# Two-layer hybrid encoder trunk on one core: an opening with a VectorE cast, another product order and shorter warming, the factor's spread in another PSUM tile, and the last stores in parts

## The chip, the core and the metric

The kernel runs on one core of one Trainium2 chip. A core has five engines with a program each: TensorE (PE) multiplies matrices into PSUM, VectorE (DVE) and ScalarE (ACT) work on whole tiles, GpSimd (POOL) does small things, and SyncE (SP) issues transfers. An engine does its instructions in the order in which they stand in its program; a semaphore makes it wait for another engine or for a DMA. The metric is the device time of one execution in microseconds (us), as a median of several runs.

## The reference, cut to what matters

Two layers, each with a mixer and a ConvGLU feed-forward part, and a root-mean-square norm before and behind each of the four sub-layers. `x` is one sequence of 512 tokens with 1024 features, in float32.

```python
for layer in range(DEPTH):                       # DEPTH = 2
    h = rms_norm(x, mix_pre_norm[layer])
    m = even_mixer(h, ...) if layer == 0 else odd_mixer(h, ...)
    x = x + rms_norm(m, mix_post_norm[layer])
    h = rms_norm(x, ffn_pre_norm[layer])
    x = x + rms_norm(conv_ffn(h, ...), ffn_post_norm[layer])
# rms_norm(t, g) = t * rsqrt(mean(t*t, features) + 1e-6) * g
# even_mixer: h @ w_in, latent attention | 2-D neighbourhood attention, @ w_out
# odd_mixer:  h @ w_in, retention both ways | long convolution by FFT, @ w_out
# conv_ffn:   (gelu(dwconv3(h @ w_gate)) * (h @ w_up)) @ w_down   (1024 -> 2816 -> 1024)
```

## The kernel before

**Layout.** `x` is held transposed: eight tiles of 128 features by 512 tokens. Every float32 operand of a large product is split in a high part (`hi`, the value rounded to the type that PE multiplies at full speed) and a low part (`lo`, what the rounding left), and `mm` issues three products for each pair: hi by hi, hi by lo, lo by hi. A product of a 128x128 stationary tile with a 128x512 moving one adds into one PSUM bank.

**Weights** come in pieces of 128x1024 (512 KB). `load_weight` has SP issue the transfer to one of two `raw` buffers, ACT cast it to `whi` and DVE subtract to `wlo`; four pairs of these exist, so three pieces can wait ready (`AHEAD = 3`). The first piece of all comes in two halves.

**Norms.** The norm's factor is not applied to the input of a projection but to its result: `stats` sums the squares over the features with products by a column of ones, VectorE adds the epsilon, POOL takes the power -0.5; the result is a factor for each token, in columns (`rcol`). `spread` turns it into a tile `Rb` in which every row holds the factors: four PE transposes into one PSUM tile, and a copy by ACT. What multiplies by `Rb` waits for that copy.

**PSUM** has eight banks, given out in turn under four names: three "pj" and two "A" take the large products, two "B" the transposes and the sums, and one "C" what is left over. A bank is written anew when its reader has finished.

**The opening** (`main`). PE first multiplies a column of ones by itself `WARM` = 14 times, with no use for the result. Then `x` and the first four weight pieces are loaded in turn, ACT and DVE scale and split `x` to `h` (`scaled`) and square it (L544; DVE sums the squares, L546), and `proj_tok` does the first projection: eight pieces `k` of the features by four token tiles, three products each.

**Between two sub-layers** `boundary` drains the last products, takes the norm behind, updates `x`, and runs the first four projections of the next sub-layer (`proj_halves`) while the norm in front of it is not ready yet. At its end (L446 to L449) it issues the `stats` for the next factor behind the last of these products, spreads the factor and copies it to `Rb`; that copy is `self.hold`, behind which later weight casts are issued.

**The odd mixer** (`mixer1`) reads that `Rb`: VectorE scales the four projections of the boundary by it (L1079), then come twelve more projections, each scaled as it ends. Between them stands the filter's `spectrum` (L1012): eight groups of six products, all into the one "C" bank. ACT copies the first four groups out (`sp`, L1033), VectorE the other four. The feed-forward parts (`ffn`) read `Rb` in the same way; the first one also permutes it (`Rp`, L875) and turns it back to columns with four small products (L878).

**Order.** The program is not written in the order in which it runs: a tile scheduler reorders each engine's instructions by its own planned times, by priorities (`high_priority`), and by `issue_after`, which keeps an instruction behind another. The last boundary writes the output: each of the eight tiles in two halves of 256 tokens, issued on SP for odd `k` and on ACT for even `k` (L397).

Of the kernel before, what the change touches and what calls it, by code (L numbers as in the profile page):

```python
# [12 lines left out]
AF = mybir.ActivationFunctionType  # L13
# [3 lines left out]
P = 128  # L17
S = 512
D = 1024
KT = D // P  # L20
# [14 lines left out]
C_MPRE, C_MPOST, C_FPRE, C_FPOST = 0, 16, 32, 48  # L35
# [169 lines left out]
class Body:  # L205
# [44 lines left out]
    def load_weight(self, n=1):  # L250
        nc = self.nc
        raw = self.wp.tile([P, 1024], F32, tag="raw", bufs=2, name=self.nm("raw"))
        hi = self.wp.tile([P, 1024], F32R, tag="whi", name=self.nm("whi"))
        lo = self.wp.tile([P, 1024], F32R, tag="wlo", name=self.nm("wlo"))
        for i in range(n):
            c = slice(i * 1024 // n, (i + 1) * 1024 // n)
            nc.sync.dma_start(raw[:, c], self.I["w"][self.wi][:, c])
            with self.tc.high_priority(WP):

                with self.tc.issue_after(self.hold) if self.hold is not None else ExitStack():  # L260
                    nc.scalar.copy(hi[:, c], raw[:, c])  # L261
                nc.vector.tensor_tensor(lo[:, c], raw[:, c], hi[:, c].bitcast(F32), ALU.subtract)  # L262
        self.wi += 1
        self.wq.append((hi, lo))
# [23 lines left out]
    def stats(self, accs, dim, n=S, e=None, out=None):  # L288
        nc = self.nc
        c = n // P  # L290
        ps = self.PS("B")
        for j in range(c):
            for a in accs:
                nc.tensor.matmul(ps[:, j:j + 1], a[:, j * P:(j + 1) * P], self.ones, start=a is accs[0], stop=a is accs[-1])  # L294
        v = self.small(4, "v")[:, :c]
        if e is None:
            nc.vector.tensor_scalar(v, ps[:, :c], 1.0 / dim, EPS, ALU.mult, ALU.add)
        else:
            nc.vector.scalar_tensor_tensor(v, ps[:, :c], 1.0 / dim, e, ALU.mult, ALU.add)
        r = self.small(4, "r")[:, :c] if out is None else out  # L300
        self.pow = nc.gpsimd.tensor_tensor(r, v, self.mhalf[:, :c], ALU.pow)
        return r
# [29 lines left out]

    def scaled(self, hl, src, g, cs):
        hi, lo = hl[0][:, cs], hl[1][:, cs]
        self.nc.scalar.activation(hi, src, AF.Copy, scale=g)
        self.nc.vector.scalar_tensor_tensor(lo, src, g, hi.bitcast(F32), ALU.mult, ALU.subtract)


# [2 lines left out]
    def boundary(self, pool, tag, x, prod, gpost, gpre, ns, ftag, perm=False, rin=None):  # L341
        nc = self.nc
# [47 lines left out]
        def update(cs, R):  # L390
            v = v3 if perm else (lambda a: a)
            for k in range(KT):
                f = fs[k][:, cs]
                nc.vector.tensor_tensor(f, f, R, ALU.mult)
                (nc.gpsimd if last and k in POOLK else nc.vector).tensor_tensor(v(f), v(f), own(k, cs), ALU.add)
                if last:
                    (nc.sync if k % 2 else nc.scalar).dma_start(self.out[k * P:(k + 1) * P, cs], f)  # L397
                    continue
                self.scaled(h[k], f, self.col(gpre + k), cs)

# [22 lines left out]
        g = products(cb)  # L423
        next(g)
        if not last:
            acc2 = new("acc2")
            h = self.new_h()
# [10 lines left out]
        g = self.proj_halves(h, ("pj", "A", "pj", "A"))  # L438
# [7 lines left out]
        with self.tc.issue_after(self.last_mm):  # L446
            with self.tc.high_priority(HP):
                self.stats([acc2], D, out=self.rcol)
            self.hold = nc.scalar.copy(self.Rb, self.spread(self.rcol, "C")).ins  # L449
        return fs, h, ps  # L450

    def gemm(self, ps, w, h, cs=slice(0, S), order=tuple(range(KT))):
# [22 lines left out]
        return ps  # L475


    def proj_tok(self, h, at={}):
        ps = [self.PS(t) for t in ("pj", "pj", "A", "A")]
        for q in range(4):  # L480
            w = self.weight()
            for kk in range(2):
                k = 2 * q + kk
                if k in at:
                    at[k]()
                for j in range(4):
                    js = slice(j * P, (j + 1) * P)
                    self.mm(ps[j], (h[k][0][:, js], h[k][1][:, js]), self.wslice(w, slice(kk * 512, kk * 512 + 512)),
                            k == 0, k == KT - 1)
        return ps  # L490

    def out_proj(self, a, order):
# [31 lines left out]
    def main(self):  # L524
# [12 lines left out]
                self.load_weight(2 if k == 0 else 1)  # L537
        h = self.new_h()
        with self.phase("l0") as p:
            for k in range(KT):  # L540
                self.scaled(h[k], x[k], self.col(C_MPRE + k), slice(0, S))
            sqs = [self.X("sq", tag="xb") for _ in range(KT)]
            for k in range(KT):
                nc.scalar.activation(sqs[k], x[k], AF.Square)  # L544
                if k:
                    nc.vector.tensor_tensor(sqs[0], sqs[0], sqs[k], ALU.add)  # L546
            x, h, pre = self.mixer0(p, h, sqs[0])
# [10 lines left out]
    def mixer0(self, p, h, acc):  # L558
# [20 lines left out]
        def value_mm(ops, v, hd, pt, start, stop):  # L579
# [4 lines left out]
        nv = []  # L584
        self.new_factor()
        pss = self.proj_tok(h, {6: lambda: self.stats([acc], D, out=self.rcol),
                                7: lambda: nc.scalar.copy(self.Rb, self.spread(self.rcol))})
        self.table = self.pow.ins
        loads()
        rcol, Rb = self.rcol, self.Rb  # L590
# [698 lines left out]
AHEAD = 3  # L1289
HP = 100  # L1290
WP = 5
WARM = 14
LATE = 7
SB = {"xa": 8, "xb": 8, "qk": 8, "t3": 8, "s": 3}
NS = 4
# [28 lines left out]
```

## Time and profile before

| | |
|---|---|
| median of three runs | 1290.13 us (1288.92 to 1290.34) |
| the profiled execution, its own time | 1291.72 us |
| its span, from the first instruction to the last | 1289.9 us |
| mean granted clock of TensorE, as a share of full speed | 0.996 |
| PE busy | 1266.4 us, 98% of the span, 6366 matmuls |
| DVE busy | 806.1 us, 62% |
| ACT busy | 588.5 us, 46% |
| DMA, mean over the span | 105 GB/s |

Busy times are those of one engine; two engines that are busy at once count twice. A matmul's record covers its whole way through the engine, so neighbouring records overlap: what a product costs in a dense stretch is the distance from one start to the next, not the length of its record. An idle time in brackets behind a row is how long the engine stood still before it, and what ended that.

### The profile page before, as it was taken

What the parts mean: (1) busy time and instruction counts of PE and PEld (TensorE: products, weight loads), DVE (VectorE), ACT (ScalarE), POOL (GpSimd) and SP (SyncE); (2) the same over time, 40 slices, a digit from 0 to 9 for tenths busy, and PEclk for the clock granted to TensorE, in tenths of its full rate; (3) what the DMA queues carried; (4) which work ended last, traced back from release to release, by engine and by line L of the source; (5) the groups of instructions that cost most, each with busy time, mean ns of one, the idle gap of its engine ahead of it and who ended that gap; (6) DMA issues with size and microseconds to landing.
All of it is one profiled execution on the core that took longest, in us unless ns stands there. A gap on an engine that the chain in (4) does not pass through costs nothing.

```text
span 1289.9 us, 16429 instructions
## 1 busy us (share of the span) xinstructions
PE 1266.4 (98%) x6366; PEld 1054.1 (82%) x6366; DVE 806.1 (62%) x1289; ACT 588.5 (46%) x953; POOL 67.1 (5%) x81
## 2 busy tenths in 40 slices
PE   9999899999999999999999999999999999999997
PEld 8887677998788788888988888778988888888886
DVE  6678897479866765322587796873875555552323
ACT  6455798556543333222443265544553333332221
POOL 1000222000000000000110000010000000000002
PEclk9999999999999999999999999999999999999998
DMA  7432012223435343333383233214243332333331
GB/s 237 131 96 81 1 34 82 85 84 99 132 127 165 131 131 98 98 114 99 113 284 112 90 119 98 66 34 131 66 132 98 98 98 94 93 95 112 99 99 66
DMA packets 43786, 135.99 MB, mean 105 GB/s; under 512 B 4955, under 2 KB 7195, under 8 KB 43196
## 3 DMA queue, kind: packets, MB, share of 16 engines
q1 hardware_dynamic: 36156, 116.52, 28.9%
q0 software_dynamic: 3664, 12.06, 2.9%
q10 hardware_dynamic: 3888, 6.36, 1.4%
q8 instruction: 50, 0.82, 0.3%
q14 instruction: 28, 0.23, 0.1%
HBM read 126.53 MB, written 8.39 MB: 105 GB/s over the span
## 4 chain that ended last, share of the span: by engine, by line
PE 89%; ACT 4%; DVE 3%; issue 2%; DMA 1%; POOL 1%; SPq 0%; ACTq 0%; DVEq 0%; POOLq 0%
PE pspj L282 17%; PE pspj L284 17%; PE pspj L283 17%; PE psA L282 10%; PE psA L284 10%; PE psA L283 10%; DMA raw<-in_w 1%; PE psB L294 1%; ACT whi L261 1%; ACT e L792 1%; DVE wlo L262 1%; PE psB L808 1%; PE psC L282 1%; PE psC L283 1%; PE psC L284 1%
## 5 line engine op out<-in xcount | busy, mean ns | idle before, releaser
L261 ACT CAST whi<-raw 128x1024 fp32r<-128x1024 f32 (+1 forms) x200 | 209.0, 1047 | 398.5 <-PE pspj L283 223.9
L262 DVE TENSOR_TENSOR wlo<-raw,whi 128x1024 fp32r<-128x1024 f32 (+1 forms) x200 | 243.6, 1220 | 214.9 <-ACT whi L261 213.2
L282 PE MATMUL pspj<-h,whi 128*128 128x512 f32 (+1 forms) x664 | 250.1, 377 | 0.6 <-DVE v L598 0.6
L284 PE MATMUL pspj<-h,wlo 128*128 128x512 f32 (+1 forms) x664 | 249.2, 375 | 0.0
L283 PE MATMUL pspj<-h,whi 128*128 128x512 f32 (+1 forms) x664 | 249.1, 375 | 0.0
L284 PE MATMUL psA<-h,wlo 128*128 128x512 f32 (+1 forms) x424 | 155.4, 367 | 0.7 <-DVE wlo L262 0.7
L282 PE MATMUL psA<-h,whi 128*128 128x512 f32 (+1 forms) x424 | 156.0, 368 | 0.0
L283 PE MATMUL psA<-h,whi 128*128 128x512 f32 (+1 forms) x424 | 155.0, 366 | 0.0
L282 PEld LDWEIGHTS pspj<-h,whi 128*128 128x128 f32 x664 | 125.3, 189 | 23.0 <-DVE v L598 1.0
L284 PEld LDWEIGHTS pspj<-h,wlo 128*128 128x128 f32 x664 | 125.4, 189 | 22.0 <-issue 0.2
L283 PEld LDWEIGHTS pspj<-h,whi 128*128 128x128 f32 x664 | 125.4, 189 | 21.8
L282 PE MATMUL pspj<-ahi,whi 128*128 128x512 f32 x308 | 121.4, 394 | 0.0
L284 PE MATMUL pspj<-ahi,wlo 128*128 128x512 f32 x308 | 120.7, 392 | 0.0
L283 PE MATMUL pspj<-alo,whi 128*128 128x512 f32 x308 | 119.5, 388 | 0.0
L284 PEld LDWEIGHTS psA<-h,wlo 128*128 128x128 f32 x424 | 79.8, 188 | 15.4 <-DVE wlo L262 1.8
L282 PEld LDWEIGHTS psA<-h,whi 128*128 128x128 f32 x424 | 80.1, 189 | 14.8 <-issue 2.6
L283 PEld LDWEIGHTS psA<-h,whi 128*128 128x128 f32 x424 | 80.0, 189 | 12.4
L892 DVE TENSOR_TENSOR t<-psA,Rb 128x512 f32<-128x512 f32 x40 | 27.6, 690 | 76.2 <-PE psA L284 76.2
L284 PEld LDWEIGHTS pspj<-ahi,wlo 128*128 128x128 f32 x308 | 57.8, 188 | 13.6
L283 PEld LDWEIGHTS pspj<-alo,whi 128*128 128x128 f32 x308 | 57.8, 188 | 12.9
L282 PEld LDWEIGHTS pspj<-ahi,whi 128*128 128x128 f32 x308 | 57.9, 188 | 11.5
L902 ACT ACTIVATE g<-g 128x512 f32<-128x512 f32 x44 | 27.7, 632 | 78.0 <-DVE g L898 40.6
(368 smaller groups left out, 2104.2 us busy)
## 6 DMA issues: line engine op xcount, KB each, us to landing
raw<-in_w SPq DMA_DIRECT2D x198, 512.0 KB, 3.5
x<-in_xT SPq DMA_DIRECT2D x16, 256.0 KB, 4.3
t<-filt POOLq DMA_DIRECT2D x16, 256.0 KB, 5.9
bias<-in_rpb POOLq DMA_DIRECT2D x8, 384.0 KB, 3.6
fflt<-in_fwin SPq DMA_DIRECT2D x8, 256.0 KB, 3.8
filt<-fh SPq DMA_DIRECT2D x8, 256.0 KB, 2.2
filt<-fl SPq DMA_DIRECT2D x8, 256.0 KB, 2.5
xspill<-f ACTq DMA_DIRECT2D x8, 256.0 KB, 3.8
```

What stands on the lines that cost most here:

```text
L261: nc.scalar.copy(hi[:, c], raw[:, c])
L262: nc.vector.tensor_tensor(lo[:, c], raw[:, c], hi[:, c].bitcast(F32), ALU.subtract)
L282: nc.tensor.matmul(ps, stat[0], mov[0], start=start, stop=False)
L283: nc.tensor.matmul(ps, stat[0], mov[1], start=False, stop=False)
L284: self.last_mm = nc.tensor.matmul(ps, stat[1], mov[0], start=False, stop=stop).ins
L294: nc.tensor.matmul(ps[:, j:j + 1], a[:, j * P:(j + 1) * P], self.ones, start=a is accs[0], stop=a is accs[-1])
L792: nc.scalar.activation(e, ps, AF.Exp, bias=nmx, accum_out=den[:, i:i + 1])
L808: nc.tensor.transpose(pt[:, i * P:(i + 1) * P], es[i][:, j * P:(j + 1) * P], self.ident)
L892: scaled = nc.vector.tensor_tensor(t, gps, Rb, ALU.mult)
L902: nc.scalar.activation(g, g, AF.Gelu_apprx_tanh)
```

## The change

Six things are changed.

1. `WARM` goes from 14 to 8.
2. The first half of the first weight piece is cast to `whi` by VectorE, not ACT, and the first tile's scaling to `h` is issued behind that cast.
3. `proj_tok` does the twelve products of `k` = 0 by parts: for all four token tiles `h`'s high part by the weight's high part, then `h`'s low part by the weight's high part, and last `h`'s high part by the weight's low part; it did the three products of one token tile together.
4. Each square of `x` on ACT is issued behind the scaling of the next tile.
5. `stats` goes over the summands in the outer loop and over the token tiles in the inner one; it was the other way round.
6. The boundary's last spread (`rcol`) goes to a "B" bank and not to "C"; the last two output tiles' second halves are stored in two pieces of 64 rows, one on SP and one on ACT.

```diff
@@ load_weight
-                    nc.scalar.copy(hi[:, c], raw[:, c])
+                    if self.wi == 0 and i == 0:
+                        self.first = nc.vector.tensor_copy(hi[:, c], raw[:, c]).ins
+                    else:
+                        nc.scalar.copy(hi[:, c], raw[:, c])
@@ stats
-        for j in range(c):
-            for a in accs:
-                nc.tensor.matmul(ps[:, j:j + 1], a[:, j * P:(j + 1) * P], self.ones, start=a is accs[0], stop=a is accs[-1])
+        for i, a in enumerate(accs):
+            for j in range(c):
+                nc.tensor.matmul(ps[:, j:j + 1], a[:, j * P:(j + 1) * P], self.ones, start=i + j == 0,
+                                 stop=i == len(accs) - 1 and j == c - 1)
@@ scaled
-        self.nc.scalar.activation(hi, src, AF.Copy, scale=g)
+        self.cast = self.nc.scalar.activation(hi, src, AF.Copy, scale=g).ins
@@ boundary, update
                 if last:
-                    (nc.sync if k % 2 else nc.scalar).dma_start(self.out[k * P:(k + 1) * P, cs], f)
+                    if k < KT - 2 or cs.start == 0:
+                        (nc.sync if k % 2 else nc.scalar).dma_start(self.out[k * P:(k + 1) * P, cs], f)
+                    else:
+                        for q, rs in ((nc.sync, slice(0, 64)), (nc.scalar, slice(64, 128))):
+                            q.dma_start(self.out[k * P + rs.start:k * P + rs.stop, cs], f[rs])
@@ boundary, its end
-            self.hold = nc.scalar.copy(self.Rb, self.spread(self.rcol, "C")).ins
+            self.hold = nc.scalar.copy(self.Rb, self.spread(self.rcol, "B")).ins
@@ proj_tok
-    def proj_tok(self, h, at={}):
+    def proj_tok(self, h, at={}, first=False):
+                ws = self.wslice(w, slice(kk * 512, kk * 512 + 512))
+                js = [slice(j * P, (j + 1) * P) for j in range(4)]
+                if k == 0 and first:
+                    for a, b in ((0, 0), (1, 0), (0, 1)):
+                        for j in range(4):
+                            self.nc.tensor.matmul(ps[j], h[k][a][:, js[j]], ws[b], start=a + b == 0, stop=False)
+                    continue
@@ main
             for k in range(KT):
-                self.scaled(h[k], x[k], self.col(C_MPRE + k), slice(0, S))
+                with ExitStack() if k else self.tc.issue_after(self.first):
+                    self.scaled(h[k], x[k], self.col(C_MPRE + k), slice(0, S))
+                casts.append(self.cast)
             for k in range(KT):
-                nc.scalar.activation(sqs[k], x[k], AF.Square)
+                with self.tc.issue_after(casts[min(k + 1, KT - 1)]):
+                    nc.scalar.activation(sqs[k], x[k], AF.Square)
@@ 
-WARM = 14
+WARM = 8
```

The scheduler moves more than the diff writes. In the rows below a row is one instruction of an engine's program (`x4`: four in a row), written as line, operation, output and inputs; the number behind a name counts allocations and so differs by six between the two kernels.

First VectorE's program in the opening, around the low part of the second weight piece: `wlo` is a weight's low part, `h` the low part of a piece of `x`, `sq` the running sum of squares. Before:

```order
L336 SCALAR_TENSOR_TENSOR h_150<-x_115,cols,h_149 128x512
L546 TENSOR_TENSOR sq_180<-sq_180,sq_182 128x512
L262 TENSOR_TENSOR wlo_119<-raw_117,whi_118 128x1024
L336 SCALAR_TENSOR_TENSOR h_152<-x_123,cols,h_151 128x512
L546 TENSOR_TENSOR sq_180<-sq_180,sq_183 128x512
L336 SCALAR_TENSOR_TENSOR h_154<-x_125,cols,h_153 128x512
```

And of the changed kernel:

```order
L341 SCALAR_TENSOR_TENSOR h_144<-x_109,cols,h_143 128x512
L566 TENSOR_TENSOR sq_174<-sq_174,sq_175 128x512
L265 TENSOR_TENSOR wlo_113<-raw_111,whi_112 128x1024
L341 SCALAR_TENSOR_TENSOR h_146<-x_117,cols,h_145 128x512
L566 TENSOR_TENSOR sq_174<-sq_174,sq_176 128x512
L341 SCALAR_TENSOR_TENSOR h_148<-x_119,cols,h_147 128x512
```

Ahead of this `wlo` the running sum has taken in the square of one tile fewer, and so from there on.

Second PE's program where the even feed-forward part begins: the spread of `rcol`, the first filter product (L974, after L994), the products of a projection into "A", and the four that turn `Rp` to columns (L878, after L898). Before:

```order
L318 MATMUL psC_3122<-ident,rcol_3016 128x128 x4
L282 MATMUL psA_3186<-h_2690,whi_2849 128x512
L283 MATMUL psA_3186<-h_2691,whi_2849 128x512
L284 MATMUL psA_3186<-h_2690,wlo_2850 128x512
L282 MATMUL psA_3186<-h_2692,whi_2849 128x512
L974 MATMUL psC_3176<-fs_3141,fs_3142 64x512
L878 MATMUL psB_3134<-ident,Rp_3132 128x1 x4
```

And of the changed kernel:

```order
L323 MATMUL psB_3116<-ident,rcol_3010 128x128 x4
L994 MATMUL psC_3170<-fs_3135,fs_3136 64x512
L285 MATMUL psA_3180<-h_2684,whi_2843 128x512
L286 MATMUL psA_3180<-h_2685,whi_2843 128x512
L898 MATMUL psB_3128<-ident,Rp_3126 128x1 x4
```

Two products of the projection stand between the spread and the turning products where four stood, and the filter product has moved ahead of them.

Third PE's program where the odd mixer begins, from the last product of the boundary's projections to the first of the next (`pspj`): `psC` with `dftfhi` and `dftflo` is the spectrum. Before:

```order
L284 MATMUL psA_6103<-h_5639,wlo_5752 128x512
L318 MATMUL psC_6024<-ident,rcol_5918 128x128 x4
L282 MATMUL psC_6140<-t_1099_6043,dftfhi 128x512
L283 MATMUL psC_6140<-t_1100_6044,dftfhi 128x512
L284 MATMUL psC_6140<-t_1099_6043,dftflo 128x512
L282 MATMUL psC_6140<-t_1101_6045,dftfhi 128x512
L283 MATMUL psC_6140<-t_1102_6046,dftfhi 128x512
L284 MATMUL psC_6140<-t_1101_6045,dftflo 128x512
L282 MATMUL pspj_6149<-h_5625,whi_5757 128x512
```

Of the changed kernel, the end of that stretch:

```order
L287 MATMUL psC_6226<-t_1105_6047,dftflo 128x512
L285 MATMUL psC_6272<-t_1103_6045,dftfhi 128x512
L323 MATMUL psB_6018<-ident,rcol_5912 128x128 x4
L286 MATMUL psC_6272<-t_1104_6046,dftfhi 128x512
L287 MATMUL psC_6272<-t_1103_6045,dftflo 128x512
L285 MATMUL psC_6272<-t_1105_6047,dftfhi 128x512
L286 MATMUL psC_6272<-t_1106_6048,dftfhi 128x512
L287 MATMUL psC_6272<-t_1105_6047,dftflo 128x512
L285 MATMUL pspj_6143<-h_5619,whi_5751 128x512
```

Three whole groups of the spectrum (6134, 6180 and 6226, six products each, back to back, with nothing else between them) and the first product of a fourth now stand ahead of the spread; before, none did, and the second to fourth group stood between products of the projections.

Last ACT's program at the same place. Before:

```order
L261 CAST whi_5757<-raw_5756 128x1024
L261 CAST whi_5763<-raw_5762 128x1024
L449 COPY Rb_5919<-psC_6024 128x512
L261 CAST whi_6105<-raw_6104 128x1024
L1086 ACTIVATE u_6079<-x_6035,cols 128x512
```

And of the changed kernel:

```order
L264 CAST whi_5751<-raw_5750 128x1024
L264 CAST whi_5757<-raw_5756 128x1024
L1053 ACTIVATE sp_6141<-psC_6134 128x512
L1053 ACTIVATE sp_6187<-psC_6180 128x512
L1053 ACTIVATE sp_6233<-psC_6226 128x512
L458 COPY Rb_5913<-psB_6018 128x512
L264 CAST whi_6099<-raw_6098 128x1024
```

The three copies that empty the spectrum's groups have moved ahead of the copy to `Rb`, and the next weight cast stands behind it.

## Rows read from the trace of the kernel before

**Rows 1.** The page, part 1: busy time of each engine.
```profile
PE 1266.4 (98%) x6366; PEld 1054.1 (82%) x6366; DVE 806.1 (62%) x1289; ACT 588.5 (46%) x953; POOL 67.1 (5%) x81
```
**Rows 2.** Waits of PE: total us, times, longest us.
```profile
PE psB L318 <- POOL r L301: 3.8, 5, 1.2
```
**Rows 3.** Timeline, 0 to 8 us: start, us, engine, line, operation.
```profile
0.93 5.71 PE L530 MATMUL psC<-ones 128*128 128x128 f32 x28 [0.93 <-DVE ones L226]
...
5.35 1.12 ACT L261 CAST whi<-raw 128x512 fp32r<-128x512 f32 x2
...
6.39 0.48 PE L282 MATMUL pspj<-whi,h 128*128 128x512 f32 x1
```
**Rows 4.** DVE, grouped by line and shape: busy us, mean ns.
```profile
L798 DVE TENSOR_SCALAR e<-e,rd 128x512 f32<-128x512 f32 x16 | 7.1, 477 | 0.1
```
**Rows 5.** Timeline, 13 to 31.2 us.
```profile
14.56 0.69 DVE L546 TENSOR_TENSOR sq<-sq,sq 128x512 f32<-128x512 f32 x1
15.16 1.22 DVE L262 TENSOR_TENSOR wlo<-raw,whi 128x1024 fp32r<-128x1024 f32 x1
...
27.51 1.05 ACT L261 CAST whi<-raw 128x1024 fp32r<-128x1024 f32 x1 [3.39 <-DMA raw<-in_w]
...
29.74 1.40 DVE L598 SCALAR_TENSOR_TENSOR v<-pspj,rcol,v 128x512 fp32r<-128x512 f32 x2
...
30.54 0.50 PE L282 MATMUL pspj<-h,whi 128*128 128x512 f32 x1 [0.56 <-DVE v L598]
```
**Rows 6.** Timeline, 287 to 291.5 us.
```profile
288.39 1.14 ACT L875 COPY Rp<-Rb 128x512 f32<-128x512 f32 x1
...
288.60 1.07 PE L974 MATMUL psC<-fs,fs 33*64 33x512 f32 x2
...
289.60 1.05 PE L878 MATMUL psB<-ident,Rp 128*128 128x1 f32 x8
```
**Rows 7.** Timeline, 667 to 676 us, and one row at 684.
```profile
668.98 0.60 PE L318 MATMUL psC<-ident,rcol 128*128 128x128 f32 x4
669.62 0.58 ACT L449 COPY Rb<-psC 128x512 f32<-128x512 f32 x1 [1.08 <-PE psC L318]
...
670.25 0.50 PE L282 MATMUL psC<-t,dftfhi 128*128 128x512 f32 x1 [0.67 <-ACT Rb L449]
...
671.75 0.39 PE L282 MATMUL pspj<-h,whi 128*128 128x512 f32 x1
...
683.90 0.68 DVE L1079 TENSOR_TENSOR cv<-pspj,Rb 128x512 f32<-128x512 f32 x1
```
**Rows 8.** Timeline, 685 to 687 us: one handover of the "C" bank.
```profile
685.00 0.39 PE L283 MATMUL psC<-t,dftfhi 128*128 128x512 f32 x1
...
685.22 0.40 PE L284 MATMUL psC<-t,dftflo 128*128 128x512 f32 x1
...
685.66 0.60 ACT L1033 ACTIVATE sp<-psC 128x512 f32<-128x512 f32 x1 [1.73 <-PE psC L284]
...
686.31 0.50 PE L282 MATMUL psC<-t,dftfhi 128*128 128x512 f32 x1 [0.46 <-ACT sp L1033]
...
686.88 0.39 PE L282 MATMUL pspj<-h,whi 128*128 128x512 f32 x1
```
**Rows 9.** Timeline, 1278 to 1290 us: the last sums and updates.
```profile
1280.29 0.36 PE L294 MATMUL psB<-ones,acc 128*128 128x1 f32 x2
...
1286.31 0.50 DVE L395 TENSOR_TENSOR f<-f,f 128x256 f32<-128x256 f32 x1
```
**Rows 10.** DMA issues, 1275 to 1290 us: KB each, median us to landing.
```profile
out<-f SPq DMA_DIRECT2D x8, 128.0 KB, 1.7
```
**Rows 11.** Timeline of PE, 842 to 850 us and 129.5 to 134 us.
```profile
845.12 0.58 PE L318 MATMUL psB<-ident,r 128*128 128x128 f32 x3 [1.21 <-POOL r L301]
...
132.99 0.50 PE L282 MATMUL pspj<-lh,whi 128*128 128x512 f32 x1 [1.45 <-DVE qf L776]
```
**Rows 12.** Windows: us, busy us of each engine (x count), PEclk (granted clock), DMA share, GB/s.
```profile
0.50:1.00 0.50, 0.07 (x1) 0.08 (x1) 0.14 (x2) 0.00 (x0) 0.20 (x1) 1.00 0.00 0
...
133.00:134.00 1.00, 1.00 (x4) 0.66 (x4) 0.79 (x4) 1.00 (x4) 0.48 (x1) 1.00 0.00 0
...
846.00:847.00 1.00, 1.00 (x5) 0.81 (x3) 0.62 (x2) 0.00 (x0) 0.00 (x0) 0.50 0.93 373
```

More of the change, by code (lines that the diff above doesn't have):

```diff
@@ L485, in proj_tok @@
                     at[k]()
+                ws = self.wslice(w, slice(kk * 512, kk * 512 + 512))
[5 more added lines that the diff above has]
+                    continue
                 for j in range(4):
-                    js = slice(j * P, (j + 1) * P)
-                    self.mm(ps[j], (h[k][0][:, js], h[k][1][:, js]), self.wslice(w, slice(kk * 512, kk * 512 + 512)),
-                            k == 0, k == KT - 1)
+                    self.mm(ps[j], (h[k][0][:, js[j]], h[k][1][:, js[j]]), ws, k == 0, k == KT - 1)
         return ps
@@ L539, in main @@
         with self.phase("l0") as p:
+            casts = []
             for k in range(KT):
-                self.scaled(h[k], x[k], self.col(C_MPRE + k), slice(0, S))
+                with ExitStack() if k else self.tc.issue_after(self.first):
+                    self.scaled(h[k], x[k], self.col(C_MPRE + k), slice(0, S))
+                casts.append(self.cast)
             sqs = [self.X("sq", tag="xb") for _ in range(KT)]
             for k in range(KT):
-                nc.scalar.activation(sqs[k], x[k], AF.Square)
+                with self.tc.issue_after(casts[min(k + 1, KT - 1)]):
+                    nc.scalar.activation(sqs[k], x[k], AF.Square)
                 if k:
@@ L586, in mixer0 @@
         pss = self.proj_tok(h, {6: lambda: self.stats([acc], D, out=self.rcol),
-                                7: lambda: nc.scalar.copy(self.Rb, self.spread(self.rcol))})
+                                7: lambda: nc.scalar.copy(self.Rb, self.spread(self.rcol))}, True)
         self.table = self.pow.ins
```

## Prediction
> **What bounds the kernel now.** I read the page's busy times first. PE is busy 98% of the span [rows 1]: 1289.9 less 1266.4 leaves 23.5 us in which it stands still. A change that takes no product away can win or lose only there, so I listed PE's waits; no releaser has more than the 3.8 us, in five waits, of one small POOL operation [rows 2]. Work on the other engines counts only where PE waits behind it. So each edit is followed to the next PE wait, in the timeline around the opening, the beginnings of the even feed-forward part and of the odd mixer, and the tail. What a product costs in a dense stretch is the distance between starts: 685.00 to 685.22, 0.22 to 0.23 us [rows 8].
>
> The sum stands against the profiled execution: span 1289.9 and 1.8 around it, 1291.72. That is 1.6 above the median of the three runs, so I move the difference over to the median, 1290.13. A change under 0.2% (2.6 us) is about what a measurement of this kernel can't tell from none: "same" is 1287.55 to 1292.71.
>
> **The opening.** PE's warming products run from 0.93 to 6.64; the first useful one starts at 6.39, overlapping the last [rows 3]. Eight of fourteen would end at about 0.93 + 8/14 x 5.71 = 4.2. The cast of the first half starts on ACT at 5.35, with no wait in its row, so the weight was there by then. On VectorE its nearest row is a copy-like operation of 128x512 at 0.48 [rows 4]; 1.12 for two on ACT says about the same. So the first product can start between 4.2 and 5.35 + 0.48 = 5.8. I take 5.3, about 1 us earlier; the order by parts keeps PE busy while `wlo` is made.
>
> That isn't the gain. PE runs on to 30, where it waits 0.56 us for `v`, released by VectorE; `v` starts at 29.74, right behind the `wlo` of the weight whose cast started at 27.51 after 3.39 us of waiting for a DMA [rows 5]. A `raw` buffer is refilled only when its `wlo` has been made, so that DMA hangs on earlier `wlo`s, and the visible one is at 15.16. Its place in VectorE's program has moved ahead by one sum of squares, which is 14.56 to 15.16 = 0.60 [rows 5]. If the chain moves by that and PE has its 1 us of slack, the restart at 30.54 comes **0.6 earlier**. Bounds: the whole 0.56 wait and another 0.8 of earlier PE go through, -1.4; or the DMAs don't land earlier and the extra cast delays VectorE, +0.2 (0.48 less about half that is covered by PE's warming). The squares deferred by one cast are off PE's path: their sum is needed only at `k` = 6; without that cover each would cost what one sum costs, 0.6.
>
> **The even feed-forward part.** After the spread PE does four products, the filter product, and at 289.60 the turning products, which wait for `Rp`: the copy runs 288.39 + 1.14 = 289.53 [rows 6]. The spread is in the same place and the copy to `Rb` too, so `Rp` comes at the same time; but two fewer products stand ahead of the turning products, and PE waits 2 x 0.23 = 0.46 longer. The filter product no longer waits for the C bank, which wins back up to 0.1 before 288.60 that is lost again in front of `Rp`. I take **+0.45**, between 0 (if the two products fall into a later wait) and +0.6.
>
> **The odd mixer.** Here most of the sum lies. Before, the spread starts at 668.98, ACT copies to `Rb` from 669.62, PE waits 0.67 for that copy because the spectrum's first group needs the same "C" bank, and goes on at 670.25; the projection starts at 671.75 [rows 7]. With the spread in a "B" bank this wait is gone, but the scheduler now puts three groups of the spectrum and the first product of a fourth ahead of the spread, all in the one "C" bank. A group may start only when ACT has emptied the one before. What that costs has a row: the last product of a group starts at 685.22, ACT copies 685.66 to 686.26, the next group starts at 686.31 [rows 8]. That is 1.09 us instead of 0.23: 0.86 lost, and the first product after such a wait takes about 0.11 more (0.50 against 0.39). There was other work between in this row (two transposes); in the new order there is none. Three handovers: 3 x (0.86 + 0.11) = **+2.9**.
>
> Removed: the wait of 0.67 at 670.25 and its slow first product, and the 0.46 before 686.31 with its slow first product [rows 7, 8], 0.78 + 0.57 = **-1.35** together, since these groups are now done.
>
> Late next: the spread. Three groups with three handovers and one product last about 7.3 us (first group 5 x 0.23 + 1.09, two more of 0.33 + 4 x 0.23 + 1.09, and the one product 0.33), so it starts at 676.3 rather than 668.98, and the copy to `Rb` at 676.9. Everything that multiplies by `Rb` on VectorE moves by 7.3 us. PE's next projection starts at about 678.3 instead of 671.75, with 18 products of the spectrum already done (18 x 0.23 = 4.1, so 2.4 behind). Before, VectorE's `cv`, which frees a "pj" bank for the third projection, ended at 684.58, that is 14.96 after `Rb` began [rows 7]. From 676.9 it ends at about 691.9, so the third projection starts there rather than at 686.88 [rows 8], 5.1 later. At that point PE has done ten products more than before (2.3): the spectrum's groups that stood behind 686.88 in the old order. 5.1 - 2.3 = **+2.8**: VectorE's delay absorbs the removed waits, which would have made it 2.9 - 1.35 = +1.55 if VectorE kept up. I take +2.8; bounds +1.0 (VectorE catches up fully, and a handover costs 0.2 less than its row) and +3.5 (the lag costs 0.7 more). ACT's weight cast behind the copy to `Rb` comes up to 7 us late; three pieces are ready ahead, 24 products or 5.5 us each, so this is covered unless two come late together.
>
> The odd feed-forward part has the same spread, in the same place, no row moved: **0**.
>
> **The tail.** The order of sums takes one pair of small products (0.36 with overlap [rows 9]) off the way from the last square to the factor: about -0.2. The halves of the last stores leave on two queues; the last update ends at 1286.81 [rows 9], the span 3.1 us later, of which 1.7 is a landing [rows 10]. Half the bytes for each can't save more than part of that; the issue on two queues saves at most one issue. I take -0.1. Together **-0.3** (-0.5 to +0.1). The Trainium skill (DMA: Bandwidth & Descriptors, "Issuing engines are not separate DMA queues") says that transfers from different engines run on the same DMA engines and only issuing time is saved; by that the stores give nothing, and the sum would be 0.1 higher. No run here shows it yet.
>
> **Sum.** -0.6 + 0.45 + 2.8 + 0 - 0.3 = +2.35: the profiled execution would take 1294.1, the median **1292.4 us**. The bounds add to -0.9 and +4.4: 1289.2 to 1294.5.
>
> **Rivals.**
> - *The new waits are given back* (0.16). Time that PE loses ahead of a wait for another engine costs nothing if that engine isn't late as well, and such waits stand further on in the mixer, those for `r` for instance [rows 2]. Then the handovers only move idle time, and the odd mixer costs nothing. Against it: VectorE and with it the later waits hang on the same `Rb`, which is itself late by 7.3 us. Then -0.6 + 0.45 - 0.3 = -0.45: 1289.7.
> - *The clock falls in the odd mixer* (0.13). After the wait of 1.21 us before 845.12 the granted clock fell to 0.50, 1.2 GHz, for the window at 846 [rows 11, 12]; at half the clock a product costs 0.22 more. Three waits of 0.9 one after the other could do the same. Against it: after 1.45 us before 132.99 the clock stayed at 1.00 [rows 11, 12]. If eight products run at that level, 8 x 0.22 = 1.8 come on top: 1292.4 + 1.8 = 1294.2, slower by 0.3%. Two such products are enough to cross the bound of 1292.71.
> - *Too little warming* (0.05). Eight warming products are followed by a pause of about 1.1 us until 5.3; if the twelve products of `k` = 0 then run at half the clock, they cost 12 x 0.22 = 2.6 more. The earlier start takes 1.0 of that and the wait of 0.56 before 30.54 another 0.56; the last 1.0 is lost, and the 0.6 isn't won: 1292.4 + 1.6 = 1294.0. Against it: the window from 0.5 us shows clock 1.00 from the first product on [rows 12]. The Trainium skill (TensorE: Matmul & The Clock Gate, Part 1) says that the default state is throttled and that activity releases it; the trace doesn't show a throttled start.
> - *The opening gives more* (0.08). Faster by over 0.2% needs -2.6: the odd mixer at nothing and the opening at -3, if the weight chain moves by a whole DMA wait (3.39 [rows 5]). Nothing shows a free DMA slot that early. About 1287.3.
>
> **How the numbers follow.** My forecast has 0.58. It ends at 1292.4, 0.3 under the bound of "slower", so I split it: 0.37 same, 0.21 slower. The first rival is same (0.16); of the clock and the warming nearly all is slower (0.17); the last is faster (0.08). Same 0.54, slower 0.38, faster 0.08. The range goes from 1289.2 (the low bound, with the first rival inside) to 1294.3 (the clock's rivals, just under the high bound).
>
> **What would show it.** First product at about 5.3, restart of PE near 29.9. Near 289 a wait of about 0.8 before the turning products. Near 671 to 676 three waits of PE for `sp`, each ending 1.09 after the last product's start, `Rb` at about 676.9, and a wait of PE for a "pj" bank or for `cv` near 690. If `cv` follows `Rb` by much less than 15 us, the +2.8 shrinks to +1.5; if the handovers are shorter than 0.8, my main term is wrong; if the clock shows under 1.00 near 672 or at 5, a rival holds.

## The result, and the profile after

The changed kernel takes 1297.06 us (median of five runs, 1295.37 to 1298.36) against 1289.69 us: a ratio of 1.0051 with a 95% interval of 1.0040 to 1.0062, that is 5 to 8 us slower. Measured again among the experiments it was 1.0048 (1.0035 to 1.0062). The prediction had the side right, 1292.4 us, but the time lies outside its range.

The profiled execution took 1297.06 us with a span of 1295.3: 5.4 us more span than the profile of before. To see where, the same product of both programs can be laid side by side and its shift read along the span:

```
behind the opening (33 us)            -0.6
238 to 247 us, products of 256 columns  +0.4
even feed-forward part (288 to 296)     +0.5
296 to 660 us, most of it near 640      +0.2
odd mixer (669 to 712)                  +2.9
905 to 917 us, a weight lands later     +0.4
944 to 956 us, a weight lands later     +0.4
sums of the last boundary (1272, 1282)  +0.3 and -0.2
from VectorE's last row to the end      +1.2
```

The page's part 1 of the changed kernel, which answers to [rows 1], shows as good as the same work:

```profile
PE 1267.4 (98%) x6354; PEld 1052.0 (81%) x6354; DVE 806.7 (62%) x1290; ACT 588.2 (45%) x952; POOL 67.7 (5%) x81
```

PE's waits, from the list of the changed kernel (total us, times, longest), name 2.2 us in three waits for the spectrum's copies, where the kernel before has one of 0.46 [rows 8], and leave the wait for POOL of [rows 2] as it was:

```profile
PE psB L323 <- POOL r L306: 3.8, 5, 1.2
PE psC L285 <- ACT sp L1053: 2.2, 3, 0.7
```

The timeline of the changed kernel in the opening answers to [rows 3, 5]. The first useful product starts at 5.29, and the restart behind the first projection at 30.08 instead of 30.54, without the wait for `v`. The `wlo` of [rows 5] starts at 15.71 instead of 15.16:

```profile
5.29 0.72 PE L501 MATMUL pspj<-whi,h 128*128 128x512 f32 x2 [0.59 <-DVE whi L262]
...
15.71 1.22 DVE L265 TENSOR_TENSOR wlo<-raw,whi 128x1024 fp32r<-128x1024 f32 x1
...
29.15 1.40 DVE L618 SCALAR_TENSOR_TENSOR v<-pspj,rcol,v 128x512 fp32r<-128x512 f32 x2
...
30.08 0.39 PE L285 MATMUL pspj<-h,whi 128*128 128x512 f32 x1
```

Where the even feed-forward part begins, the answer to [rows 6]: `Rp` is 0.12 earlier than before, since the whole program is, and PE now waits for it.

```profile
288.23 1.18 ACT L895 COPY Rp<-Rb 128x512 f32<-128x512 f32 x1
...
289.47 1.05 PE L898 MATMUL psB<-ident,Rp 128*128 128x1 f32 x8 [0.23 <-ACT Rp L895]
```

Where the odd mixer begins, the answer to [rows 7, 8]. Each group of the spectrum waits for the copy of the one before; the spread starts at 676.86 and the copy to `Rb` at 677.49, where they were at 668.98 and 669.62; the third projection starts when the `cv` ahead of it has ended, 691.73 + 0.68 = 692.41:

```profile
671.08 0.60 ACT L1053 ACTIVATE sp<-psC 128x512 f32<-128x512 f32 x1 [2.02 <-PE psC L287]
...
671.73 0.50 PE L285 MATMUL psC<-t,dftfhi 128*128 128x512 f32 x1 [0.69 <-ACT sp L1053]
...
674.13 0.50 PE L285 MATMUL psC<-t,dftfhi 128*128 128x512 f32 x1 [0.75 <-ACT sp L1053]
...
676.52 0.50 PE L285 MATMUL psC<-t,dftfhi 128*128 128x512 f32 x1 [0.74 <-ACT sp L1053]
676.86 0.60 PE L323 MATMUL psB<-ident,rcol 128*128 128x128 f32 x4
...
677.49 0.59 ACT L458 COPY Rb<-psB 128x512 f32<-128x512 f32 x1 [1.03 <-PE psB L323]
...
678.95 0.47 PE L285 MATMUL pspj<-h,whi 128*128 128x512 f32 x1 [0.34 <-DVE x L1099]
...
691.73 0.68 DVE L1099 TENSOR_TENSOR cv<-pspj,Rb 128x512 f32<-128x512 f32 x1
...
692.47 0.50 PE L285 MATMUL pspj<-h,whi 128*128 128x512 f32 x1
```

And the tail, the answer to [rows 9]: the four last products of ones stand together, but behind VectorE's last instruction, which ends at 1291.02, SP still issues two stores one after the other, and the span ends 4.3 us later instead of 3.1.

```profile
1284.47 0.60 PE L298 MATMUL psB<-ones,sq 128*128 128x1 f32 x4 [0.47 <-ACT sq L363]
...
1290.52 0.50 DVE L400 TENSOR_TENSOR f<-f,f 128x256 f32<-128x256 f32 x1
1290.76 0.51 SPq L406 DMA_DIRECT2D out<-f  x1
1290.77 1.42 ACTq L406 DMA_DIRECT2D out<-f  x2
1291.37 0.54 SPq L403 DMA_DIRECT2D out<-f  x1
1292.00 0.49 SPq L406 DMA_DIRECT2D out<-f  x1
```

### The profile page after: what moved, and what is told of

Same layout as the page of the kernel before. It is cut to its first block, busy times and chain, and to the rows that moved or that the text cites. A ratio compares the mean times of both kernels' runs of the same rounds, so it can differ in the third digit from the quotient of the medians.

```text
span 1295.3 us, 16421 instructions
## 1 busy us (share of the span) xinstructions
PE 1267.4 (98%) x6354; PEld 1052.0 (81%) x6354; DVE 806.7 (62%) x1290; ACT 588.2 (45%) x952; POOL 67.7 (5%) x81
## 4 chain that ended last, share of the span: by engine, by line
PE 88%; ACT 4%; DVE 2%; issue 2%; DMA 2%; POOL 1%; ACTq 0%; SPq 0%; POOLq 0%; DVEq 0%
PE pspj L285 17%; PE pspj L287 17%; PE pspj L286 17%; PE psA L285 11%; PE psA L287 10%; PE psA L286 10%; DMA raw<-in_w 1%; PE psB L298 1%; ACT whi L264 1%; ACT e L812 1%; PE psB L828 1%; PE psC L285 1%; DVE wlo L265 1%; POOL r L306 1%; PE psC L286 1%
```

## The experiments

The theory: the loss is the spread's new place in PE's order (3 us in the odd mixer, 0.5 ahead of it) and the stores in parts (1.2). The rivals: the opening or the sums cost something later, the mixer's shift is given back, or the B bank itself costs. Single traces of kernels with the same stretch differ by up to 2.2 us, so a stage is read where several traces show it.

**The change without the spread, without the stores, without both.**

```diff
e1  -self.spread(self.rcol, "B")        e2  -for q, rs in ((nc.sync, slice(0, 64)), ...
e1  +self.spread(self.rcol, "C")        e2  +(nc.sync if k % 2 else nc.scalar).dma_start(...)
e3  both
```

> The change with the boundary's spread put back into the C bank; all else as changed. If the odd mixer's new order (three groups handed over through one bank, spread and Rb 7 us late) is the main loss, then this takes away 3.0 us there and 0.5 at the even feed-forward part: about 3.5 us faster than the changed kernel, 0.4 to 1.5 us slower than the kernel before, and no wait of PE for sp of 0.7 near 672 to 677 remains. Rival: the loss comes from the opening, the order of the sums or the stores, and the mixer's shift is given back further on; then this stays within 1 us of the changed kernel.

> The change with whole stores for the last two output tiles, as before. If issues on two queues at once lengthen each other and delay the last piece, then the stretch from VectorE's last instruction to the end of the span goes from 4.3 back to 3.1 us, and the kernel is 1.2 us faster than the changed one, 2.7 to 4.0 us slower than the kernel before. Rival: the end is set by the landing of the last bytes alone, whatever their pieces; then the stretch stays above 4 us.

> The change with the spread in C and with whole stores: only the opening and the order of the sums are left. If spread and stores hold the whole loss, this is 0.8 us faster to 0.3 us slower than the kernel before, with PE's restart near 30 about 0.6 us earlier. Rival: the opening or the sums cost something that the profile doesn't show as a wait of PE (slower weight transfers further on); then it is 1 to 3 us slower than the kernel before.

Measured against the kernel before: e1 1.0007 (0.9998 to 1.0016), e2 1.0037 (1.0023 to 1.0051), e3 0.9991 (0.9982 to 1.0000). The spread back in C takes off some 5.7 us (0.51% less 0.07%), more than the 3.5 expected; whole stores take off about 1.8; both together bring the kernel to 1289.02 us, 1.2 us under the kernel before and the best version run, though the interval ends at no change. From VectorE's last end to the span's end e1 shows 4.3 us and e2 3.1. The rivals that blame the opening or the sums for a loss fall.

**The B bank with the old order.** The spectrum's products are planned behind the spread's last transpose; whole stores.

```diff
-            self.hold = nc.scalar.copy(self.Rb, self.spread(self.rcol, "B")).ins
+            self.hold = nc.scalar.copy(self.Rb, self.spread(self.rcol, "B")).ins
+            self.spreads = self.turn               # the last transpose
...
+                    with self.tc.issue_after(self.spreads):
                         self.mm(ps, (mats[0][:, m, hh, c], mats[1][:, m, hh, c]), sd[hh], hh == 0, hh == 1)
```

> The change with whole stores, and with the spectrum's products planned behind the spread's last transpose, so that the spread is in a B bank and PE's order in the odd mixer is that of before. If the order costs and not the bank, then PE has neither the three waits for sp nor the wait of 0.67 for Rb: about 3.6 us faster than the change with whole stores alone, and 1.2 us faster to 0.2 us slower than the kernel before. Rival: the B bank itself costs (transposes and sums wait for it); then it is as slow as the change with whole stores, 2.7 to 4.0 us over before.

1.0018 (1.0007 to 1.0028): 2.5 us faster than e2 by the ratios, but 2.3 us slower than the kernel before, where at most 0.2 was expected. Its trace has no shift in the odd mixer (+0.14 at 660, +0.09 at 760), where e2's rises by 3.0. So there the order costs and not the bank. What the trace loses stands elsewhere: 0.5 at the even feed-forward part, where the spread is still in B, 0.4 at the products of 256 columns, and weights that land later (below). Nor is the 0.67 won that PE no longer waits for `Rb`: the shift goes to -0.8 at 670, is -0.3 at 690 and back at +0.1 by 745 us. A part of it goes at the next handover:

```profile
669.11 0.60 PE L323 MATMUL psB<-ident,rcol 128*128 128x128 f32 x4
...
686.02 0.50 PE L285 MATMUL psC<-t,dftfhi 128*128 128x512 f32 x1 [0.69 <-ACT sp L1051]
```

The wait for `sp` there was 0.46 in [rows 8].

**The spread alone, at all three boundaries and at one each**, in the kernel before.

```diff
e4   -self.spread(self.rcol, "C")   +self.spread(self.rcol, "B")
e11  +self.spread(self.rcol, "B" if tag == "qk" else "C")     # ahead of the even feed-forward part
e12  +self.spread(self.rcol, "B" if perm else "C")            # ahead of the odd mixer
```

> The kernel before with one thing changed: the boundary's last spread goes to a B bank. If the spread's tile is the main loss by the order that it makes, then this alone is 3.5 to 5 us slower than the kernel before: 3.0 in the odd mixer (three waits for sp of 0.7, Rb 7 us later), 0.5 at the even feed-forward part, and up to 1 more from weights that land 0.4 later further on, as in all three runs with the B bank so far. Rival: it needs the changed opening to be late; then under 1.5 us.

> The kernel before with the spread in a B bank only at the boundary ahead of the even feed-forward part, where two products instead of four stand ahead of the small products that wait for Rp. By the trace of the changed kernel this costs 0.5 us; where the granted clock falls behind the new waits, as it did in two of four executions with this order, 1.5 us come on top. So 0.5 to 2.0 us slower than the kernel before, with the difference from 288 us on and none at 671. Rival: the fall of the clock near 290 was chance and not this order's; then at most 0.6 us.

> The kernel before with the spread in a B bank only at the boundary ahead of the odd mixer. Three waits for sp of 0.7, Rb 7.3 us later, and 3.0 us slower than the kernel before, all of it between 669 and 712 us. Rival: part of that is given back further on, at the waits for r between 820 and 880; then under 2 us.

Ratios: 1.0031 (1.0019 to 1.0042), 1.0007 (0.9999 to 1.0016), 1.0020 (1.0010 to 1.0029), so 4.0, 0.9 and 2.6 us. The shifts in the traces: in the odd mixer +3.1 (e4) and +3.0 (e12), at the even feed-forward part +0.5 (e11) and +2.1 (e4). e12's list of PE's waits:

```profile
PE psC L282 <- ACT sp L1033: 2.5, 4, 0.7
```

**Where the clock falls.** In e4 and in e2 the even feed-forward part has 1.5 us on top. Windows of e2 (us, then busy us of PE, PEld, DVE, ACT, POOL, then the granted clock, DMA share, GB/s):

```profile
291.00:292.00 1.00, 1.00 (x9) 1.00 (x10) 0.10 (x1) 1.00 (x2) 0.00 (x0) 1.00 0.00 0
292.00:293.00 1.00, 1.00 (x4) 0.82 (x5) 0.97 (x3) 1.00 (x2) 0.00 (x0) 0.72 0.00 0
293.00:294.00 1.00, 1.00 (x3) 0.79 (x3) 1.00 (x2) 0.92 (x2) 0.00 (x0) 0.50 0.00 0
294.00:295.00 1.00, 1.00 (x4) 0.75 (x3) 1.00 (x2) 0.20 (x1) 0.00 (x0) 0.50 0.00 0
295.00:296.00 1.00, 1.00 (x4) 0.81 (x3) 1.00 (x4) 0.42 (x1) 0.00 (x0) 0.57 0.64 94
```

Eight products there run 0.43 apart, at 1.2 GHz. PE had stood still for 0.40 us before 288.39 and for 0.24 before 290.94. The fall came in two of six traces with the spread in B at this place (the changed kernel twice, e2, e4, e6, e11) and in none of the twelve others. e11 shows the order's own 0.5 and no fall, so that the fall is this order's is likely, not shown.

Falls come without this order too. Every trace has the waits of [rows 11], about 1.45 us near 132 and 1.21 near 845; behind the first the clock fell in eleven of the eighteen traces (0.1 to 0.3 us lost, 1.2 in e2, where the fall lasted twice as long), behind the second in nine (1.5 us lost). The window of e10 that answers to the one at 133 in [rows 12]:

```profile
134.00:135.00 1.00, 1.00 (x6) 0.89 (x5) 1.00 (x2) 0.00 (x0) 1.00 (x1) 0.50 0.00 0
```

**The stores.** e5 is the kernel before with the stores of the change; e8 the change with the spread in C and both halves of a tile on one queue; e10 the kernel before with only the last store halved, both on SP; e15 the same cut by tokens.

```diff
e8   for rs in (slice(0, 64), slice(64, 128)): q.dma_start(self.out[k * P + rs.start:k * P + rs.stop, cs], f[rs])   # q: SP for odd k, ACT for even
e10  the same for k == KT - 1 alone
e15  for i in range(2): q.dma_start(self.out[k * P:(k + 1) * P, cs.start + i * P:...], f[:, i * P:(i + 1) * P])
```

> The kernel before with only the stores of the last two output tiles in parts. 1.2 us slower than the kernel before; the stretch from VectorE's last instruction to the end of the span is 4.3 us instead of 3.1. Rival: under 0.3 us, if the issues are delayed only because the changed kernel's other edits bring the last tiles together.

> The change with the spread in C, and with both halves of a tile on one queue: tile 6 on ACT's, tile 7 on SP's, so that the half stores of a tile follow each other and seldom meet one of the other queue. If two issues at the same time lengthen each other, an issue takes 0.33 to 0.35 here where it took 0.49 to 0.78, and the stretch from VectorE's last instruction to the end of the span is 3.4 to 3.6 us. Rival: a piece of 64 rows takes longer by itself; then each issue still takes 0.5 or more and the stretch stays above 3.9 us.

> The kernel before with only the very last store (tile 7, second half) in two pieces of 64 rows, both on SP's queue; the second is issued when no other queue issues. If two issues at the same time lengthen each other, the second piece's issue takes 0.33 and the stretch from VectorE's last instruction to the end of the span is 3.3 to 3.5 us. If a piece of 64 rows takes longer by itself, both issues take 0.5 and the stretch is 3.8 us or more.

> The kernel before with the very last store in two pieces of 128 rows by 128 tokens, both on SP's queue, instead of two of 64 rows by 256 tokens. If the 64 rows make an issue long, each issue takes 0.33 here and the stretch from VectorE's last instruction to the end of the span is 3.3 to 3.5 us. If any extra piece of the last tile takes long, the issues take 0.5 or more and the stretch is 3.8 us or more.

e5: 1.0009 (1.0000 to 1.0018), the end 4.2 us behind VectorE. e8: 1.0004 (0.9994 to 1.0013), 3.9 us; the queues met again, so its time at the end told nothing apart. e10: 1.0008 (0.9998 to 1.0019), 3.9 us. e15, with one execution, 3.3 us. The rows on the tile `out` (duration in ns of an issue, least, median, most), first of e10, then of e15:

```profile
L402 SPq DMA_DIRECT2D out<-f x2: 513/550/588, 1285.4 to 1286.0; - x2
```

```profile
L402 SPq DMA_DIRECT2D out<-f x2: 333/388/442, 1284.4 to 1284.8; - x2
```

Pieces of 64 rows take 0.51 and 0.59 us to issue though no other queue issues at the second; whole rows by half the tokens take 0.33 and 0.44. So a piece of 64 rows takes longer without a collision of queues; this rests on one trace of each kernel. The landing is longer too, 2.0 to 2.5 us for the halves of the change against 1.7 in [rows 10]. In e8 halves that met took 0.51 to 0.63, hardly more. But in the changed kernel, while both queues issue, a whole store takes 0.54 and a half one 0.77, and nothing run here explains these two.

**The opening.** e9 is the changed opening alone, e13 the same with 14 warming products; e16 and e17 are a further execution of each.

```diff
e9   before + cast on VectorE, products by parts, squares deferred, WARM = 8
e13  -WARM = 8   +WARM = 14
```

> The kernel before with the changed opening only (cast on VectorE, products by parts, squares deferred, 8 warming products); sums, spread and stores as before. If the opening is worth the 0.6 to 0.7 us that the traces keep behind 60 us, this is 0.4 to 1.5 us faster than the kernel before, equal to the kernel with opening and sums; its tail has the three pairs of small products again (0.2 us more there, 0.25 less near 1272). Rival: the order of the sums holds the gain; then it is within 0.3 us of the kernel before.

> The changed opening alone, but with 14 warming products again. If PE's earlier start isn't the gain and the chain of weight casts is, PE's first useful product starts near 6.4 us, a little after the cast on VectorE would allow, and PE's restart behind the first projection is as early as with eight (0.3 to 2.2 us earlier than in the kernel before): equal to the opening alone within 0.3 us. Rival: PE's earlier start is the gain; then this ties with the kernel before.

> The changed opening alone once more, for a second trace of it with 8 warming products. If PE's earlier start is the gain, PE is 0.5 to 1.5 us earlier than with 14 at 20 us and behind its restart near 30 us, as in the first trace. Rival: the restart is set by when the weights land, which differs from execution to execution; then the two counts of warming products don't sort the traces.

> The changed opening alone with 14 warming products once more, beside the trace with 8. If PE's earlier start is the gain, PE's products near 20 us stand within 0.6 us of the kernel before's and so does the restart near 30. Rival: the restart comes 0.6 us or more earlier, as the chain of casts would make it.

By time e9 and e13 tie with the kernel before and each other: 0.9996 (0.9988 to 1.0005) and 0.9996 (0.9987 to 1.0005). The traces say more, though not firmly. The same product behind the restart (33 us), against the profile of before: nine traces with eight warming products stand 0.1 to 2.3 us earlier, 1.2 in the mean; six others with the old opening 0.1 to 0.9 earlier, 0.5 in the mean; the two with fourteen 0.55 later and 0.42 earlier. So by the traces the opening is worth about 0.7 us, and only with PE's earlier start; but that rests on two traces with fourteen, and the times, good to about 1.2 us, don't tell fourteen from eight. In most traces PE reaches the restart without a wait: the one for `v` [rows 5] stands in three of the eighteen (before 0.56, e12 0.47, e13 0.60), so where PE is early, it stays early. The earlier start doesn't always hold: e16's first products, after the cut in warming, run at half pace, 0.43 apart, as two more of the nine traces do (e2, and e8 for some of its first products); and e16's restart is 0.1 earlier only. PE's timeline of e16, and its window from 6 us, whose granted clock reads 1.00 all the same:

```profile
5.38 1.19 PE L495 MATMUL pspj<-whi,h 128*128 128x512 f32 x2 [0.68 <-DVE whi L262]
6.37 1.05 PE L495 MATMUL psA<-whi,h 128*128 128x512 f32 x2
7.23 1.05 PE L495 MATMUL pspj<-whi,h 128*128 128x512 f32 x2
```

```profile
6.00:7.00 1.00, 1.00 (x4) 0.81 (x3) 0.65 (x2) 0.62 (x1) 0.00 (x0) 1.00 0.98 361
```

With fourteen, e13:

```profile
6.43 0.71 PE L495 MATMUL pspj<-whi,h 128*128 128x512 f32 x2
6.98 0.62 PE L495 MATMUL psA<-whi,h 128*128 128x512 f32 x2
```

The 1.00 in e16's window is not a reading of the clock. The trace's own list of granted clocks begins at 9.45 us in e16, at 9.14 in e2, at 6.68 in e8 and between 3.8 and 5.4 in the six others with eight, each time with the full level; ahead of its first entry a window shows 1.00. The products tell what the clock was there: where the list begins, e16's go from 0.43 apart to 0.23, and in the profile of before the warming passes (two for each product) go from 0.21 apart to 0.11 at 5.81. In all eighteen traces the warming begins with 0.21. So every traced execution starts at the lower level, 1.2 GHz, and with eight products the first useful ones can come before it has risen.

**The whole change again.**

> The changed kernel once more, beside runs of the kernel before on the chip of the experiments. The parts measured alone (opening with sums -0.09%, spread +0.31%, stores +0.09%) add to 0.31%, 4.0 us; the changed kernel measured 0.51%. If the parts add, this is 3 to 5.5 us slower than the kernel before, more where the clock falls near 290 us. Rival: the edits work on each other (the opening or the stores cost more beside the spread's new order); then it is 6 us or more again.

1.0048 (1.0035 to 1.0062), 6.2 us: nearer the rival's number, though the interval, 4.5 to 8.0 us, reaches into the first range. The parts measured alone add to 4.0 us (-0.09, 0.31 and 0.09%), with intervals that allow 2 us either way, so whether the edits work on each other is open. What e14's trace shows besides the parts is the late weights, below.

**Weights that land later.** Near 910 and 943 us a weight's transfer ends a wait of ACT. ACT's row behind the second, first before, then of the changed kernel, both with the transfer issued 2.3 us ahead of the spread:

```profile
942.80 1.05 ACT L261 CAST whi<-raw 128x1024 fp32r<-128x1024 f32 x1 [0.62 <-DMA raw<-in_w]
```

```profile
947.03 1.05 ACT L264 CAST whi<-raw 128x1024 fp32r<-128x1024 f32 x1 [1.11 <-DMA raw<-in_w]
```

4.27 us from issue to cast became 4.77. At the first place PE waits behind it, first before, then in the changed kernel:

```profile
913.05 0.35 PE L294 MATMUL psB<-ones,acc 128*128 128x1 f32 x2 [0.64 <-DVE acc L360]
```

```profile
916.80 0.58 PE L298 MATMUL psB<-ones,acc 128*128 128x1 f32 x4 [1.03 <-DVE acc L365]
```

Against the profile of before, PE loses 0.4 to 1.9 us by the two places in five of the eighteen traces (the changed kernel twice, e2, e6 and e8); the twelve others are 0.3 to 1.2 us earlier there, so the profile of before is late itself. Its transfer issued near 905 took 4.32 us to land, 4.4 to 5.0 in the five, 3.5 to 4.2 in the twelve. e4 has the B bank and lands on time, e8 has C and lands late, e1 differs from e8 by the queue of the stores alone and lands on time. All five have the changed order of the sums, as have e1 and e3, which land on time; no kernel with the old order is as late. That rival was not run alone, and the cause is open.

## Why the prediction was wrong, step by step

- **The odd mixer** was right: +2.8 forecast, +2.9 in the profile, 3.0 and 3.1 in e12 and e4. Its steps hold too, 0.5 us later by what came ahead: three waits of 0.69 to 0.75, the copy to `Rb` at 677.49 (676.9 forecast), the third projection 5.1 late after that shift, held by the `cv` as said. The rival that the waits are given back fell.
- **The even feed-forward part**: +0.45 forecast, +0.5 in the profile. The wait is 0.23 and not the 0.8 that I named; the loss is that two fewer products stand in the same stretch, from the spread to the turning products (287.08 to 289.60 before, 286.93 to 289.47 now). What was missing is the fall of the clock behind it. The rival of the falling clock had the right price, 1.5 to 1.8 us, but the wrong place: I looked for it at the mixer's three waits, which kept 1.00 in every trace. The row that I held against it, 1.00 behind the wait near 133, was that execution's: eleven of eighteen fall there.
- **The opening**: -0.6 forecast and measured, but that is luck. The `wlo` that was to come 0.6 earlier came 0.5 later (15.71), and by 20 us PE's earlier start was used up (+0.25 against before). The -0.6 is there because PE has no wait for `v`, and that wait was a chance of the one trace that I read: fifteen of eighteen lack it. "That isn't the gain" is doubtful too: I took PE's earlier start for slack and the sum of squares moved ahead in VectorE's program for the gain, but with fourteen warming products and that same order neither trace is earlier than those of the old opening; the times leave it open. The rival of too little warming came true in three of nine traces. What I held against it, a clock of 1.00 from the first product on, was no reading of the clock: the warming passes 0.21 apart show a start at the lower level. The rule of the Trainium skill (TensorE: Matmul & The Clock Gate, Part 1), that the default state is throttled and that activity releases the throttle, agrees with all eighteen traces.
- **The tail** is the step that failed in sign: -0.3 forecast, of which -0.1 for the stores; measured -0.2 for the sums and +1.2 for the stores. I priced a half store as at most a whole one; it takes 0.5 to 0.8 us to issue where the whole one takes 0.33, and the last of them follows another on SP. The order of the sums also costs 0.2 to 0.3 near 1272 and 0.14 near 640 in all seven traces that have it, places that I didn't look at.
- **Not in the sum**: weights that land later, +0.8 in this profile, and 0.4 between 238 and 247 us, where the same products of 256 columns run 0.118 apart instead of 0.114; seven of the experiments' traces, with and without the spread in B, show that one too. They lie outside what the diff touches.
- **The base**: the profiled execution of before, 1.6 us above its median, holds two waits that are shorter or missing in most traces, the 0.56 for `v` near 30 and the 0.64 at 913. Its fall of the clock near 846 stands in the changed kernel's profile too (848) and cancels. I moved the difference over as it stood. The changed kernel's median is at its profile, so 5.3 us between the profiles became 6 to 7 between the medians.

The bounds that I gave the tail (-0.5 to +0.1) were the main fault in the range: the edit had no row of its size, and I bounded it by the transfer's saving alone. With the measured +1.2 the upper bound is 1295.6, still short of 1297.06; the rest is the weights and the products of 256 columns, whose cause no run shows, and the base.

## What to carry to other kernels

A bank that is moved frees one wait, but what a scheduler then puts ahead counts: read each engine's new order, find the resource that the moved groups share, and price each handover by a row; this part came out to 0.2 us. For an operation whose size no row shows (a store of half the rows), the bound must reach to a loss as well, since a smaller piece need not be cheaper. Where waits are added, a fall of the clock can follow in some executions only, and it belongs into the price with its share. A wait, or a clock that holds, in one trace may be that execution's: look at a second trace before its removal is priced or a rival is dismissed by it.

## What the runs showed of the hardware

- A store of 64 rows by 256 tokens takes 0.49 to 0.78 us to issue and 2.0 to 2.5 to land, one of 128 rows with the same tokens 0.33 and 1.7 (0.54 and 2.0 between two halves), one of 128 rows by 128 tokens 0.33 to 0.44 and 1.6.
- After short stops of PE the granted clock falls to 0.50 for some 3 us in some executions and not in others of the same order: near 290 in two of six, near 132 in eleven and near 846 in nine of eighteen traces.
- TensorE starts at the lower level in all eighteen traces and rises between 3.8 and 9.5 us; a window ahead of the rise prints 1.00 all the same, and the distance between products shows the level.
